# Where the four weight sums of a Strassen-Winograd down projection are made: in SBUF beside the products, or in DRAM by background transfers

## The chip, the cores and the metric

One core of a Trainium2 chip. The metric is the device time of one execution in microseconds, median of three runs; the profile is one more execution with the hardware profiler on.

## The reference

One layer on 512 tokens of width 1024, float32. A projection `h @ w_in` feeds three token mixers (gated linear attention, GLA; a causal pooling mixer; block-sparse attention, MoBA), whose outputs go through branch matrices and gates into `w_out`. Then the FFN, which is what the change is about:

```
f = (silu(h @ ffn_w_gate) * (h @ ffn_w_up)) @ ffn_w_down      # 512x1024 -> 512x2816 -> 512x1024
x = x + rmsnorm(f, norm_ffn_post)
```

## The kernel before

**Matrix products.** Each float32 operand is split into two float32r tiles, H (the rounded value, a copy on ScalarE) and L (the rest, a subtraction on VectorE), and a product is the three matmuls HH, HL, LH, accumulated in PSUM. A weight chunk of 512 KB passes through three rings of buffers: `load` (L143) allocates a buffer of `raw` (3 of them), a DMA on SyncE's queue fills it, ScalarE makes `wH` and VectorE `wL` (4 buffers each; `split_chunk`, L136). These four are marked as urgent by `LEAD`, so they run ahead of the matmuls that use them as far as the rings allow.

**Order.** The program is traced in the order of the text; a planner then puts the instructions of each engine into one fixed queue, by the text's order, the urgency marks and its own reckoning of when operands are there. At run time each engine takes its queue in order and waits where an operand is missing. Only the start (norm of x, first projections) has an order of VectorE, ScalarE and TensorE written by hand; GpSimd has there four powers for the norms (L228) and one subtraction (L326). Two GpSimd memsets of the GLA stage stand under `issue_after(pows[3].ins)`, which ties them behind the last of the four powers. In the GLA stage GpSimd squares each output (`osq`, L606) and takes a power (L610) on which VectorE's L613 waits.

**Stages in time.** Start to 30 us; projections, GLA, MoBA, pooling and branches to 432; `w_out` to 478; FFN (11 steps of 96 matmuls for gate and up) to 720; down projection to 837; the last norm and stores to 845.

**The down projection.** The product of `g` (512 x 2816) and W_down (2816 x 1024) is made as 2 x 2 quarters by the Strassen-Winograd scheme: seven products p1 to p7 of quarter size instead of eight. Quarter (z, c) of W_down has rows z*1408 on and columns c*512 on; it is loaded in six chunks (five of 2 x 128 rows, one of 128; `wq`, L885). Four of the products need a sum of quarters: t1 = (0,0) + (0,1), t2 = t1 + (1,1), t3 = (1,1) + (0,1), t4 = t2 + (1,0). The kernel before makes them so:

- t1: in the FFN stage SyncE loads (0,0) into the SBUF tiles `tau` and GpSimd issues DMAs that add (0,1) to them on landing (`plus`, L892; text at FFN steps 3 to 8).
- t2 and t4: the same tiles, by further accumulating DMAs (`t2_of`, `t4_of`), each of which waits until the splits of the sum before have read the tile.
- t3: two plain loads per chunk and an addition on VectorE (L993, L994).

The products are computed in the order p1, p2, p5, p6, p7, p3, p4 (`product`, L922). Before each, the quarter of `g` (or a sum of quarters, L972 to L988) is split by `Quarter.put` (L871). p1, p2 and p3 load their quarters into `raw` (`raw_of`, L944, L948); p5, p6 and p4 split straight from `tau`, p7 from the `t3` tiles.

Of the kernel before, what the change touches and what calls it, by code (L numbers as in the profile page):

```python
# [9 lines left out]
F32 = mybir.dt.float32  # L10
# [3 lines left out]
ALU = mybir.AluOpType  # L14
AX = mybir.AxisListType

P = 128
T = 512
# [49 lines left out]
LEAD = 400  # L68
G1W = RANK + 256
TH = T // 2  # L70
KH = NF // 2
KGROUPS = ((0, 4), (4, 8), (8, KH))
# [3 lines left out]
def hybrid_block(ctx: ExitStack, tc: tile.TileContext, a: dict, out: bass.AP):  # L76
    nc = tc.nc
    V, S, G, PE = nc.vector, nc.scalar, nc.gpsimd, nc.tensor
# [6 lines left out]
    dram = ctx.enter_context(tc.tile_pool(name="dram", bufs=1, space=bass.MemoryType.DRAM))  # L85
# [8 lines left out]
    def slot(shape, name, dt=F32):  # L94
        n = int(np.prod(shape[1:]))
        if n > D or dt != F32:
            i = free_full.pop(0)
            owner[name] = (i, None, 0)
            return big.tile(shape, dt, tag=f"S{i}", name=name, bufs=1)
        if free_half:  # L100
            i, t, lo = free_half.pop(0)
        else:
            i, lo = free_full.pop(0), 0
            t = big.tile([P, 2 * D], F32, tag=f"S{i}", name=f"two_{name}", bufs=1)
            free_half.append((i, t, D))
        owner[name] = (i, t, lo)
        ap = t[:, lo:lo + n]
        names = "abcd"[:len(shape) - 1]
        if len(shape) > 2:
            ap = ap.rearrange(f"p ({' '.join(names)}) -> p {' '.join(names)}",  # L110
                              **{c: k for c, k in zip(names, shape[1:])})
        return ap

    def free(*names):
        for name in names:
            i, t, lo = owner.pop(name)
            other = (i, t, D - lo)
            if t is None:
                free_full.append(i)
            elif other in free_half:  # L120
                free_half.remove(other)
                free_full.append(i)
            else:
                free_half.append((i, t, lo))
# [8 lines left out]
        return bass.AP(tensor=vec.tensor, offset=vec.offset, ap=[[0, P], [1, n]])  # L133


    def split_chunk(src, kt, nf, H, L, name, eng, lead):  # L136
        with tc.high_priority(offset=lead):
            raw = wpool.tile([P, kt, nf], F32, tag="raw", name=f"raw_{name}", bufs=NRAW)
            nc.sync.dma_start(raw, src.rearrange("(k p) f -> p k f", p=P))
            S.copy(H, raw)  # L140
            (eng or V).tensor_tensor(L, raw, H.bitcast(F32), op=ALU.subtract)  # L141

    def load(src, name, eng=None, lead=LEAD, keep=False):  # L143


        K, nf = src.shape[0] // P, src.shape[1]
        kt = 4 if nf == G1W else D // nf
        out = []
        for c in range(K // kt):
            if keep:  # L150
                HL = slot([P, 2, kt, nf], f"{name}_{c}", F32R)
                h, l = HL[:, 0], HL[:, 1]
            else:
                h = wpool.tile([P, kt, nf], F32R, tag="wH", name=f"wH_{name}_{c}", bufs=NWH)
                l = wpool.tile([P, kt, nf], F32R, tag="wL", name=f"wL_{name}_{c}", bufs=NWH)
            split_chunk(src[c * kt * P:(c + 1) * kt * P, :], kt, nf, h, l, f"{name}_{c}", eng, lead)
            out.append((h, l, c * kt, kt))
        return out
# [286 lines left out]
    gq, gk = gqk[:, 0], gqk[:, 1]  # L445
# [415 lines left out]
    def quarter(tz, z, i):  # L861
        return ga[z, i][:, :, tz * TH:(tz + 1) * TH]
# [15 lines left out]
        def free(self):  # L878
            free(*self.names)

    wd = a["ffn_w_down"]
    chunks = [(lo, min(lo + 2, KH)) for lo in range(0, KH, 2)]
    NG = range(len(KGROUPS))

    def wq(z, c, lo, hi):  # L885

        r = (z * KH + lo) * P
        return wd[r:r + (hi - lo) * P, c * T:(c + 1) * T].rearrange("(k p) f -> p k f", p=P)

    tau = [slot([P, hi - lo, T], f"tau{n}") for n, (lo, hi) in enumerate(chunks)]  # L890

    def plus(n, name, z, c, dst):  # L892

        nc.gpsimd.dma_start(dst, wq(z, c, *chunks[n]), accum_op=ALU.add)  # L894

    a11 = Quarter("a11")
    for u in range(NF // 2):
        W = [load(a[n][:, u * 256:(u + 1) * 256], f"{n}{u}") for n in ("ffn_w_gate", "ffn_w_up")]
        ff = [ps2((2 * u + f) % 4, f"ff{2 * u + f}") for f in range(2)]
        for lo, hi in (((0, 256), (256, 512)) if u == 0 else ((0, 512),)):  # L900
            for i in range(2):
                mm_fm([g[i][:, lo:hi] for g in ff], W[i], h2, lo, hi)
        if 3 <= u < 3 + len(chunks):
            nc.sync.dma_start(tau[u - 3], wq(0, 0, *chunks[u - 3]))
            plus(u - 3, "t1", 0, 1, tau[u - 3])
        for f in range(2):
            k = 2 * u + f
            z, r = divmod(k, KH)
            sg = t2(f"sg{k}")
            S.activation(sg, ff[f][0], AF.Silu)  # L910
            V.tensor_tensor(ga[z, r // 4][:, r % 4, :], sg, ff[f][1], op=ALU.mult)
            if z == 0 and r + 1 in [hi for _, hi in KGROUPS]:
                a11.put(r // 4, quarter(0, 0, r // 4))
    h2.free()

# [3 lines left out]
    def product(name, X, ps, src, start, group=1):  # L922

        done = []
        for n, (lo, hi) in enumerate(chunks):
            with tc.high_priority(offset=LEAD):
                w = src(n)
                h = wpool.tile([P, 2, T], F32R, tag="wH", name=f"wH_{name}{n}", bufs=NWH)[:, 0:hi - lo]
                l = wpool.tile([P, 2, T], F32R, tag="wL", name=f"wL_{name}{n}", bufs=NWH)[:, 0:hi - lo]
                S.copy(h, w)  # L930
                V.tensor_tensor(l, w, h.bitcast(F32), op=ALU.subtract)  # L931
            done.append((lo, hi, h, l))
            if n + 1 < len(chunks) and n >= len(chunks) - group:
                continue
            for j in range(2):
                for lo_, hi_, h_, l_ in done:
                    for k in range(lo_, hi_):
                        for i, (z, w_) in enumerate(((0, h_), (0, l_), (1, h_))):
                            PE.matmul(ps[j], lhsT=X.part(z, k, j), rhs=w_[:, k - lo_, :],  # L939
                                      start=start and k == 0 and i == 0, stop=k == KH - 1 and i == 2,  # L940
                                      skip_group_check=True)
            done = []

    def raw_of(z, c, name):  # L944
        def src(n):
            lo, hi = chunks[n]
            r = wpool.tile([P, 2, T], F32, tag="raw", name=f"raw_{name}{n}", bufs=NRAW)[:, 0:hi - lo]
            nc.sync.dma_start(r, wq(z, c, lo, hi))  # L948
            return r
        return src  # L950

    def t1_of(n):
        return tau[n]

    def t2_of(n):
        plus(n, "t2", 1, 1, tau[n])
        return tau[n]

    def t3_of(n):
        return t3[n]  # L960

    def t4_of(n):
        plus(n, "t4", 1, 0, tau[n])
        return tau[n]

    pa, pc, pd, pe = (ps2(i, f"p{i}") for i in range(4))
    a12 = Quarter("a12")
    for i in NG:
        a12.put(i, quarter(0, 1, i))
    s1 = [slot([P, hi - lo, TH], f"s1_{i}") for i, (lo, hi) in enumerate(KGROUPS)]  # L970
    for i in NG:
        V.tensor_tensor(s1[i], quarter(1, 1, i), quarter(1, 0, i), op=ALU.subtract)  # L972
    product("p1", a11, pa, raw_of(0, 0, "p1"), True)
    cp0 = slot([P, 2, T], "c_p")
    for j in range(2):
        S.copy(cp0[:, j], pa[j])
# [1 line left out]
    qs1 = Quarter("qs1_")  # L978
    for i in NG:
        qs1.put(i, s1[i])  # L980
    product("p2", a12, pd, raw_of(1, 0, "p2"), True)
    for j in range(2):
        V.tensor_tensor(cp0[:, j], pd[j], cp0[:, j], op=ALU.add)

# [2 lines left out]
        V.scalar_tensor_tensor(quarter(0, 0, i), s1[i], -1.0, quarter(0, 0, i), ALU.mult, ALU.subtract)  # L987
        V.scalar_tensor_tensor(quarter(0, 1, i), quarter(0, 0, i), -1.0, quarter(0, 1, i), ALU.mult, ALU.subtract)  # L988
    a12.free()
    t3 = [slot([P, hi - lo, T], f"t3_{n}") for n, (lo, hi) in enumerate(chunks)]  # L990
    for n in range(len(chunks)):
        with tc.high_priority(offset=LEAD):
            nc.sync.dma_start(t3[n], wq(1, 1, *chunks[n]))  # L993
            V.tensor_tensor(t3[n], t3[n], raw_of(0, 1, "t3")(n), op=ALU.add)  # L994
    product("p5", qs1, pc, t1_of, True)
    qs1.free()
    qs2 = Quarter("qs2_")
    for i in NG:
        qs2.put(i, quarter(0, 0, i))
    free(*[f"s1_{i}" for i in NG])  # L1000
    product("p6", qs2, pa, t2_of, False)
    qs2.free()
    qs3 = Quarter("qs3_")
    for i in NG:
# [3 lines left out]
    for j in range(2):  # L1008
        S.copy(cp1[:, j], pa[j])
        V.scalar_tensor_tensor(cp1[:, j], pc[j], -1.0, cp1[:, j], ALU.mult, ALU.subtract)  # L1010
    product("p7", qs3, pa, t3_of, False)
    qs4 = Quarter("qs4_")
    for i in NG:
        qs4.put(i, quarter(0, 1, i))
# [1 line left out]
        S.copy(cp2[:, j], pa[j])  # L1016
        V.scalar_tensor_tensor(cp2[:, j], pc[j], -1.0, cp2[:, j], ALU.mult, ALU.subtract)
    qs3.free()
    free(*[f"t3_{n}" for n in range(len(chunks))])
    product("p3", qs4, pe, raw_of(1, 1, "p3"), True)  # L1020
    a22 = Quarter("a22")
    for i in NG:
        a22.put(i, quarter(1, 1, i))
# [17 lines left out]

    for t in range(2):
        finish(t, [cp0[:, t], cp1[:, t]], (0, 1))
    product("p4", a22, pa, t4_of, False, 2)
    for t in range(2):
        finish(2 + t, [pa[t], cp2[:, t]], (1, 0))

# [26 lines left out]
```

## Time and profile before

| | |
|---|---|
| Median of 3 runs | 847.97 us (847.27 to 849.46) |
| Profiled execution | 846.82 us, its span 845.1 us |
| Busy, share of the span | TensorE 97%, VectorE 55%, ScalarE 39%, GpSimd 10% |
| Mean granted TensorE clock | 0.994 |
| DMA | 101.09 MB, mean 120 GB/s |

A share of busy time is a mean over stages with different limits, so the stages are read one by one. In the rows further on, PE is TensorE, PEld its weight loads, DVE VectorE, ACT ScalarE, POOL GpSimd, SP SyncE; SPq and POOLq are their queues of DMA issues. In an order of time a row has its start, its duration, engine, line, operation, out<-in, shape, count, and in brackets how long the engine stood idle before and what ended that. q1 is the DMA queue of SyncE, q0 that of GpSimd. Matmuls are pipelined: a single duration overlaps the next one.

### The profile page before, as it was taken

To read this page: it belongs to the slowest core of one execution; us is meant where nothing else is said; L and a number is where in the kernel's file an instruction comes from. 1 tells how busy PE (TensorE), PEld (TensorE's weight loads), DVE (VectorE), ACT (ScalarE), POOL (GpSimd) and SP (SyncE) were. 2 spreads that over 40 slices of the span, in tenths; PEclk is the share of its full clock that TensorE was granted. 3 is DMA by queue.
4 is the path that set the end of the run, shared out by engine and by line. 5 is a ranking of instruction groups with operands and counts; after the bars stand their busy time and mean duration, and the time that the engine had idled before them with its cause. 6 is when DMAs were issued, how large, how long until landed. Compare 5 with 4: busy or idle time off the path is not lost.

```text
span 845.1 us, 10322 instructions
## 1 busy us (share of the span) xinstructions
PE 821.0 (97%) x4082; PEld 694.8 (82%) x4082; DVE 461.6 (55%) x680; ACT 328.3 (39%) x496; POOL 84.1 (10%) x79
## 2 busy tenths in 40 slices
PE   6999999999999999999999999999999999996996
PEld 5888998889888877888888898888888888775785
DVE  5639967766577564334455633233323323976776
ACT  6345235454456332223344332222222222543553
POOL 3200002110010003112111120000000000012201
PEclk9999999999999999999999999999999999998999
DMA  8431221222322632333343893333333332399912
GB/s 299 125 100 51 76 75 51 74 75 72 91 75 72 217 100 75 100 100 100 99 156 120 229 229 94 97 99 100 100 99 100 93 96 89 109 251 270 263 63 100
DMA packets 77395, 101.09 MB, mean 120 GB/s; under 512 B 3730, under 2 KB 57763, under 8 KB 77347
## 3 DMA queue, kind: packets, MB, share of 16 engines
q1 hardware_dynamic: 72834, 91.78, 35.1%
q0 software_dynamic: 4512, 8.65, 5.7%
q8 instruction: 32, 0.52, 0.3%
q14 instruction: 17, 0.13, 0.0%
HBM read 96.23 MB, written 4.19 MB: 119 GB/s over the span
## 4 chain that ended last, share of the span: by engine, by line
PE 91%; DMA 4%; DVE 3%; issue 1%; ACT 0%; SPq 0%; DVEq 0%; POOLq 0%; POOL 0%; ACTq 0%
PE ff L192 28%; PE p L939 7%; PE pga L192 5%; PE pgb L192 5%; PE ow L203 5%; PE pgc L192 5%; PE mv L203 3%; PE gv L203 3%; PE pya L192 3%; PE mq L192 3%; PE pu L192 3%; PE pyb L192 3%; PE mk L192 3%; PE gqk L192 3%; PE pyc L192 3%; DMA two_t<-in_ffn_w_down_dram 2%
## 5 line engine op out<-in xcount | busy, mean ns | idle before, releaser
L141 DVE TENSOR_TENSOR wL_ffn_w_gate<-raw_ffn_w_gate,wH_ffn_w_gate 128x1024 fp32r<-128x1024 f32 x22 | 26.9, 1225 | 82.4 <-ACT wH_ffn_w_gate L140 82.2
L192 PE MATMUL ff<-h2L,wH_ffn_w_gate 128*128 128x512 f32 (+1 forms) x192 | 71.4, 372 | 0.0
L192 PE MATMUL ff<-h2L,wH_ffn_w_up 128*128 128x512 f32 (+1 forms) x192 | 71.4, 372 | 0.0
L192 PE MATMUL ff<-h2H,wL_ffn_w_up 128*128 128x512 f32 (+1 forms) x192 | 71.4, 372 | 0.0
L192 PE MATMUL ff<-h2H,wL_ffn_w_gate 128*128 128x512 f32 (+1 forms) x192 | 71.3, 372 | 0.0
L192 PE MATMUL ff<-h2H,wH_ffn_w_gate 128*128 128x512 f32 (+1 forms) x192 | 71.3, 372 | 0.0
L192 PE MATMUL ff<-h2H,wH_ffn_w_up 128*128 128x512 f32 (+1 forms) x192 | 71.2, 372 | 0.0
L939 PE MATMUL p<-wH_p,qs 128*128 128x512 f32 x176 | 56.3, 400 | 1.9 <-ACT wH_p L930 1.6
L140 ACT CAST wH_ffn_w_up<-raw_ffn_w_up 128x1024 fp32r<-128x1024 f32 x22 | 23.2, 1052 | 73.5 <-issue 35.3
L141 DVE TENSOR_TENSOR wL_ffn_w_up<-raw_ffn_w_up,wH_ffn_w_up 128x1024 fp32r<-128x1024 f32 x22 | 27.0, 1225 | 43.8 <-ACT wH_ffn_w_up L140 43.7
L894 POOL DMA_DIRECT2D two_tau<-in_ffn_w_down_dram x18 | 21.1, 1254 | 289.3 <-DVE wL_p L931 276.6
L140 ACT CAST wH_ffn_w_gate<-raw_ffn_w_gate 128x1024 fp32r<-128x1024 f32 x22 | 23.2, 1053 | 61.0 <-PE ff L192 53.1
L939 PEld LDWEIGHTS p<-wH_p,qs 128*128 128x128 f32 x176 | 34.1, 194 | 9.8 <-ACT wH_p L930 2.1
L939 PE MATMUL p<-wL_p,qs 128*128 128x512 f32 x88 | 35.7, 405 | 6.4 <-DVE wL_p L931 6.4
L192 PEld LDWEIGHTS ff<-h2L,wH_ffn_w_gate 128*128 128x128 f32 x192 | 36.2, 188 | 6.2
L192 PEld LDWEIGHTS ff<-h2L,wH_ffn_w_up 128*128 128x128 f32 x192 | 36.2, 188 | 6.2
L192 PEld LDWEIGHTS ff<-h2H,wH_ffn_w_gate 128*128 128x128 f32 x192 | 36.1, 188 | 6.3
L192 PEld LDWEIGHTS ff<-h2H,wH_ffn_w_up 128*128 128x128 f32 x192 | 36.1, 188 | 6.3
L192 PEld LDWEIGHTS ff<-h2H,wL_ffn_w_up 128*128 128x128 f32 x192 | 36.2, 188 | 6.2
L192 PEld LDWEIGHTS ff<-h2H,wL_ffn_w_gate 128*128 128x128 f32 x192 | 36.2, 188 | 6.2
L939 PE MATMUL p<-wH_p,a 128*128 128x512 f32 x132 | 41.0, 390 | 0.0
L939 PEld LDWEIGHTS p<-wH_p,a 128*128 128x128 f32 x132 | 24.8, 188 | 5.1
(338 smaller groups left out, 2080.5 us busy)
## 6 DMA issues: line engine op xcount, KB each, us to landing
raw_ffn_w_gate<-in_ffn_w_gate_dram SPq DMA_DIRECT2D x22, 512.0 KB, 3.8
raw_ffn_w_up<-in_ffn_w_up_dram SPq DMA_DIRECT2D x22, 512.0 KB, 3.8
two_tau<-in_ffn_w_down_dram POOLq DMA_DIRECT2D x15, 512.0 KB, 9.5
raw_p<-in_ffn_w_down_dram SPq DMA_DIRECT2D x15, 512.0 KB, 3.9
raw_gatea<-in_w_in_dram SPq DMA_DIRECT2D x8, 512.0 KB, 3.6
raw_gateb<-in_w_in_dram SPq DMA_DIRECT2D x8, 512.0 KB, 3.6
raw_gatec<-in_w_in_dram SPq DMA_DIRECT2D x8, 512.0 KB, 3.7
raw_wo<-in_w_out_dram SPq DMA_DIRECT2D x8, 512.0 KB, 3.4
```

Source lines behind the costliest of these rows:

```text
L140: S.copy(H, raw)
L141: (eng or V).tensor_tensor(L, raw, H.bitcast(F32), op=ALU.subtract)
L192: PE.matmul(ps, lhsT=w[:, k, f * P:(f + 1) * P], rhs=m(k0 + k, lo, hi), start=n == 0 and i == 0, stop=n == len(W) - 1 and i == len(seq) - 1)
L203: PE.matmul(ps, lhsT=m(k0 + k, lo, hi), rhs=w[:, k, c0:c1], start=first and n == 0 and i == 0, stop=last and n == len(W) - 1 and i == len( ...
L894: nc.gpsimd.dma_start(dst, wq(z, c, *chunks[n]), accum_op=ALU.add)
L939: PE.matmul(ps[j], lhsT=X.part(z, k, j), rhs=w_[:, k - lo_, :], start=start and k == 0 and i == 0, stop=k == KH - 1 and i == 2, skip_group ...
```

## The change

The four sums become DRAM tiles, `sums[t, n]`. A generator, `background`, lists 48 DMAs on GpSimd's queue: for each sum six copies DRAM to DRAM (of a quarter of W_down, or of an earlier sum) and then six accumulating transfers that add the other quarter, in the order t1, t3, t2, t4. Every call of `load` but those for gq and gk draws one of them ahead of its own instructions: 34 calls of the mixer stages, 2 of `w_out`, 12 of the FFN. No urgency mark and no `issue_after` stands around them. In the down projection all seven products load plainly into `raw`, four of them from the sums; `tau`, `t3`, L994 and the accumulations into SBUF are gone. The splits of a12 move into the FFN loop, beside those of a11.

```diff
+    sums = {(t, n): dram.tile([(hi - lo) * P, T], F32, name=f"sum{t}_{n}")
+            for t in (1, 2, 3, 4) for n, (lo, hi) in enumerate(chunks)}
+
+    def background():
+        for t, first, second in ((1, (0, 0), (0, 1)), (3, (1, 1), (0, 1)), (2, 1, (1, 1)), (4, 2, (1, 0))):
+            for n in range(len(chunks)):
+                src = sums[first, n] if type(first) is int else wq(*first, *chunks[n])
+                yield nc.gpsimd.dma_start(sums[t, n], src)
+            for n in range(len(chunks)):
+                yield nc.gpsimd.dma_start(sums[t, n], wq(*second, *chunks[n]), accum_op=ALU.add)
+
+    behind = background()
...
     def load(src, name, eng=None, lead=LEAD, keep=False):
+        if not name.startswith(("gq", "gk")):
+            next(behind, None)
         K, nf = src.shape[0] // P, src.shape[1]
...
-    tau = [slot([P, hi - lo, T], f"tau{n}") for n, (lo, hi) in enumerate(chunks)]
-
-    def plus(n, name, z, c, dst):
-
-        nc.gpsimd.dma_start(dst, wq(z, c, *chunks[n]), accum_op=ALU.add)
-
-    a11 = Quarter("a11")
+    a11, a12 = Quarter("a11"), Quarter("a12")
...
-        if 3 <= u < 3 + len(chunks):
-            nc.sync.dma_start(tau[u - 3], wq(0, 0, *chunks[u - 3]))
-            plus(u - 3, "t1", 0, 1, tau[u - 3])
...
-            if z == 0 and r + 1 in [hi for _, hi in KGROUPS]:
-                a11.put(r // 4, quarter(0, 0, r // 4))
+            if r + 1 in [hi for _, hi in KGROUPS]:
+                (a11, a12)[z].put(r // 4, quarter(0, z, r // 4))
...
-    def t2_of(n):
-        plus(n, "t2", 1, 1, tau[n])
-        return tau[n]
...
+    def sum_of(t, name):
+        return raw_of(lambda n: sums[t, n], name)
...
-    a12 = Quarter("a12")
-    for i in NG:
-        a12.put(i, quarter(0, 1, i))
...
-    t3 = [slot([P, hi - lo, T], f"t3_{n}") for n, (lo, hi) in enumerate(chunks)]
-    for n in range(len(chunks)):
-        with tc.high_priority(offset=LEAD):
-            nc.sync.dma_start(t3[n], wq(1, 1, *chunks[n]))
-            V.tensor_tensor(t3[n], t3[n], raw_of(0, 1, "t3")(n), op=ALU.add)
-    product("p5", qs1, pc, t1_of, True)
+    product("p5", qs1, pc, sum_of(1, "p5"), True)
...
-    product("p6", qs2, pa, t2_of, False)
+    product("p6", qs2, pa, sum_of(2, "p6"), False)
...
-    product("p7", qs3, pa, t3_of, False)
+    product("p7", qs3, pa, sum_of(3, "p7"), False)
...
-    product("p4", a22, pa, t4_of, False, 2)
+    product("p4", a22, pa, sum_of(4, "p4"), False, 2)
```

## Rows read from the trace of the kernel before

**Rows 1.** The page's first part: busy us, share, instructions of TensorE.
```profile
PE 821.0 (97%) x4082; PEld 694.8 (82%) x4082; DVE 461.6 (55%) x680; ACT 328.3 (39%) x496; POOL 84.1 (10%) x79
```

**Rows 2.** Stretches: length; busy PE, PEld, DVE, ACT, POOL; clock; DMA share; GB/s.
```profile
0.00:25.00 25.00, 16.94 (x107) 16.16 (x108) 14.78 (x29) 15.15 (x31) 11.06 (x14) 1.00 0.77 265
25.00:50.00 25.00, 25.00 (x124) 20.82 (x122) 11.01 (x18) 7.83 (x11) 0.76 (x1) 1.00 0.48 136
50.00:116.00 66.00, 66.00 (x463) 61.41 (x463) 54.80 (x70) 30.11 (x36) 0.00 (x0) 1.00 0.20 57
488.00:720.00 232.00, 232.00 (x1082) 194.59 (x1081) 73.79 (x71) 63.96 (x74) 3.95 (x4) 1.00 0.38 106
```

**Rows 3.** TensorE's waits behind 600 us (total, times, longest); the first.
```profile
PE p L939 <- DVE wL_p L931: 7.6, 4, 4.2
PE p L939 <- ACT wH_p L930: 1.6, 1, 1.6
739.67 0.50 PE L939 MATMUL p<-wL_p,a 128*128 128x512 f32 x1 [1.25 <-DVE wL_p L931]
```

**Rows 4.** Stretches of 6 us in the down projection, columns as above.
```profile
734.00:740.00 6.00, 4.75 (x20) 3.36 (x19) 6.00 (x7) 5.62 (x7) 0.00 (x0) 1.00 0.42 139
776.00:782.00 6.00, 3.17 (x8) 2.50 (x9) 6.00 (x7) 0.78 (x1) 1.25 (x2) 0.56 1.09 273
782.00:788.00 6.00, 6.00 (x25) 4.91 (x24) 5.10 (x6) 3.23 (x4) 4.53 (x4) 0.87 1.02 216
806.00:812.00 6.00, 6.00 (x28) 4.99 (x27) 5.78 (x7) 4.36 (x7) 0.00 (x0) 1.00 0.66 218
```

**Rows 5.** VectorE's waits, 720 to 845 us, and one addition in time.
```profile
DVE two_t L994 <- DMA two_t<-in_ffn_w_down_dram: 6.5, 2, 3.9
DVE two_t L994 <- DMA raw_t<-in_ffn_w_down_dram: 6.3, 3, 4.4
775.28 1.23 DVE L994 TENSOR_TENSOR two_t<-two_t,raw_t 128x1024 f32<-128x1024 f32 x1 [3.91 <-DMA two_t<-in_ffn_w_down_dram]
```

**Rows 6.** DMA queues from 738 to 800 us: GpSimd's queue (packets, MB, share).
```profile
q0 software_dynamic: 3008, 5.77, 52.0%
```

**Rows 7.** DMA queues over the whole span (the page).
```profile
q1 hardware_dynamic: 72834, 91.78, 35.1%
q0 software_dynamic: 4512, 8.65, 5.7%
```

**Rows 8.** The products' plain loads (KB, us to landing); one copy.
```profile
raw_p<-in_ffn_w_down_dram SPq DMA_DIRECT2D x15, 512.0 KB, 3.9
739.04 1.05 ACT L930 CAST wH_p<-raw_p 128x1024 fp32r<-128x1024 f32 x1
```

**Rows 9.** SyncE's queue in order of time, from the start.
```profile
6.61 0.38 SPq L139 DMA_DIRECT2D raw_gq<-in_w_in_dram  x1
12.33 0.38 SPq L795 DMA_DIRECT2D pw<-in_pool_w_dram  x1
```

**Rows 10.** GpSimd's waits (total, times, longest); two places in time.
```profile
POOL rs_m L228 <- DVE ms_m L226: 10.1, 3, 5.0
POOL wL_g1r L326 <- ACT wH_g1r L324: 3.2, 1, 3.2
116.44 1.04 POOL L606 TENSOR_TENSOR osq<-osb 128x512 f32<-128x512 f32 x1 [90.67 <-ACT osb L605]
490.23 2.12 POOL L894 DMA_DIRECT2D two_tau<-in_ffn_w_down_dram  x2 [0.37 <-issue]
```

**Rows 11.** Line 894, the accumulations: ns min/median/max, and landing.
```profile
L894 POOL DMA_DIRECT2D two_tau<-in_ffn_w_down_dram x18: 899/1203/1691, 463.3 to 785.8; - x18
DMA to landing us min/median/max: 5.6/9.4/12.1
```

**Rows 12.** The last chain's first piece; ScalarE's copy of gq.
```profile
2.58 5.78 DMA raw_g1r<-in_w_in_dram
18.10 1.04 ACT L140 CAST wH_gq<-raw_gq 128x1024 fp32r<-128x1024 f32 x1
```

More of the change, by code (lines that the diff above doesn't have):

```diff
@@ L133, in rows, with wq @@
         return bass.AP(tensor=vec.tensor, offset=vec.offset, ap=[[0, P], [1, n]])
+    wd = a["ffn_w_down"]
+    chunks = [(lo, min(lo + 2, KH)) for lo in range(0, KH, 2)]
+    def wq(z, c, lo, hi):
+        r = (z * KH + lo) * P
+        return wd[r:r + (hi - lo) * P, c * T:(c + 1) * T]
+    sums = {(t, n): dram.tile([(hi - lo) * P, T], F32, name=f"sum{t}_{n}")
[8 more added lines that the diff above has]
+    behind = background()
     def split_chunk(src, kt, nf, H, L, name, eng, lead):
@@ L879, in free @@
             free(*self.names)
-    wd = a["ffn_w_down"]
-    chunks = [(lo, min(lo + 2, KH)) for lo in range(0, KH, 2)]
     NG = range(len(KGROUPS))
-    def wq(z, c, lo, hi):
-        r = (z * KH + lo) * P
-        return wd[r:r + (hi - lo) * P, c * T:(c + 1) * T].rearrange("(k p) f -> p k f", p=P)
-    tau = [slot([P, hi - lo, T], f"tau{n}") for n, (lo, hi) in enumerate(chunks)]
-    def plus(n, name, z, c, dst):
-        nc.gpsimd.dma_start(dst, wq(z, c, *chunks[n]), accum_op=ALU.add)
-    a11 = Quarter("a11")
+    a11, a12 = Quarter("a11"), Quarter("a12")
     for u in range(NF // 2):
@@ L942, in product, with raw_of @@
             done = []
-    def raw_of(z, c, name):
+    def raw_of(ap_of, name):
         def src(n):
@@ L947, in src, with quarter_of @@
             r = wpool.tile([P, 2, T], F32, tag="raw", name=f"raw_{name}{n}", bufs=NRAW)[:, 0:hi - lo]
-            nc.sync.dma_start(r, wq(z, c, lo, hi))
+            nc.sync.dma_start(r, ap_of(n).rearrange("(k p) f -> p k f", p=P))
             return r
         return src
-    def t1_of(n):
-        return tau[n]
-    def t2_of(n):
-        plus(n, "t2", 1, 1, tau[n])
[L957 to L964, printed above, removed]
+    def quarter_of(z, c, name):
+        return raw_of(lambda n: wq(z, c, *chunks[n]), name)
+    def sum_of(t, name):
+        return raw_of(lambda n: sums[t, n], name)
     pa, pc, pd, pe = (ps2(i, f"p{i}") for i in range(4))
-    a12 = Quarter("a12")
-    for i in NG:
-        a12.put(i, quarter(0, 1, i))
     s1 = [slot([P, hi - lo, TH], f"s1_{i}") for i, (lo, hi) in enumerate(KGROUPS)]
@@ L972, in hybrid_block @@
         V.tensor_tensor(s1[i], quarter(1, 1, i), quarter(1, 0, i), op=ALU.subtract)
-    product("p1", a11, pa, raw_of(0, 0, "p1"), True)
+    product("p1", a11, pa, quarter_of(0, 0, "p1"), True)
     cp0 = slot([P, 2, T], "c_p")
@@ L980, in hybrid_block @@
         qs1.put(i, s1[i])
-    product("p2", a12, pd, raw_of(1, 0, "p2"), True)
+    product("p2", a12, pd, quarter_of(1, 0, "p2"), True)
     for j in range(2):
@@ L1018, in hybrid_block @@
     qs3.free()
-    free(*[f"t3_{n}" for n in range(len(chunks))])
-    product("p3", qs4, pe, raw_of(1, 1, "p3"), True)
+    product("p3", qs4, pe, quarter_of(1, 1, "p3"), True)
     a22 = Quarter("a22")
```

## The prediction

> **What bounds the kernel now.** The first thing to read is the share of busy time: TensorE has 97% of the span [rows 1]. The number of matmuls does not change, so all that can be won is time in which TensorE waits or is clocked down. I looked for it stage by stage with a table of stretches [rows 2]: from 25 us on TensorE is busy without a break at a granted clock of 1.00, up to the end of the FFN at 720 us (three such stretches stand there). What is left is the start, which waits for loads, and the down projection. There the list of waits gives 7.6 us in four waits for VectorE's splits and 1.6 us in one for ScalarE's [rows 3]. Behind the longest, of 4.2 us, the clock is granted at 0.56 for 6 us and 0.87 for the next 6 [rows 4]; an undisturbed stretch of 6 us holds 28 matmuls, so the 8 + 25 matmuls there are worth 33 x 6/28 = 7.1 us and took 3.17 + 6.00 = 9.2: 2.1 us. The down projection has 9.2 + 2.1 = 11.3 us to give, and no other stage behind the start anything.
>
> The reader should see two causes in it. The first wait (1.25 us at 739, the one for ScalarE soon behind) falls where VectorE is busy 6.00 of 6 us [rows 3, 4]: its own work. At the later ones it is idle for much of the time, and its waits say why: the additions for t3 (L994) stand 6.5 + 6.3 = 12.8 us before loads that have not landed [rows 5], and the splits (L931) that TensorE needs are queued behind them. The DMA share is then above 1.0 [rows 4], and more than half of it is the 12 accumulating transfers [rows 6].
>
> **The change, part by part.**
>
> *Down projection, removed.* The additions L994 (five of 1.23 us and a half one [rows 5], 6.8 us of VectorE) and the accumulating transfers of t2 and t4: 5.77 MB at 52.0% of 62 us, 32 us of all 16 engines [rows 6]. As plain loads, which go at 91.78 MB in 35.1% of 845.1 us, 309 GB/s [rows 7], they are 19 us. The three later waits and the clock dip go: 7.6 - 1.25 + 2.1 = 8.5 us. The other two (2.9 us) stay: up to there VectorE loses only splits of a12, which now go into the FFN, where it is 32% busy [rows 2], and of those one group waits for the last FFN tile in any case.
>
> *Down projection, added.* p5, p6, p7 and p4 now load through the ring of three raw buffers. A load lands in 3.9 us (median) and its copy takes 1.05 [rows 8]; its subtraction takes what an addition of L994 takes, 1.23: 6.2 us per buffer, 2.1 us per chunk with three. TensorE needs 12 matmuls per chunk, 12 x 6/28 = 2.6 us. So the ring holds, with 0.5 us per chunk to spare; p3 already runs so, with TensorE at 6.00 of 6 us in the slice that begins at 806 [rows 4]. But p5's loads now stand behind p2's, whose buffers VectorE frees late. Cost between 0 and the 2.9 us that the two waits show for such lateness; I take 1.0. Gain of the down projection: 8.5 - 1.0 = 7.5 us (bounds 4 to 11).
>
> *The background transfers: where will they run?* There are 48 on GpSimd's queue: four sums of six copies and six accumulations. In the text one goes with each load from gv on. The trace says that the text's position holds no instruction back. pw (L795) stands behind sixteen loads that would each carry a transfer, is used only in the pooling mixer, and is issued at 12.33 us [rows 9]. On GpSimd the accumulations of t1 stand in the text at FFN steps 3 to 8; step 3 begins 8 steps of 96 matmuls, 8 x 96 x 6/28 = 165 us, before 720; the last of them are issued at 490 us [rows 10], when their loads had landed. An instruction is issued when its engine is free and its inputs are there. The copies read inputs only and write fresh DRAM tiles. GpSimd stands idle before the start's powers 10.1 us in three pieces (5.0, 3.2, 1.9) and 3.18 us before the split [rows 10], and an issue holds it 1.20 us [rows 11]: 4 + 2 + 1 + 2 = 9 transfers before the last power at 19 us. I take this: the background begins at the start, not in the mixer.
>
> *Its price at the start.* No row shows a DRAM to DRAM transfer. Nearest rows per 512 KB: the plain 309 GB/s, 1.70 us of the 16 engines, and the accumulations' 8.65 MB in 5.7% of 845.1 us, 179 GB/s, 2.92 us [rows 7]. In the first 25 us the engines are busy 77% [rows 2], so nine transfers push 15 to 26 us of work into a stretch with 5.7 us free. What TensorE waits for there is loads: the chain begins with the first weight load, 5.78 us [rows 12]. Cover: gq's first chunk is issued at 6.61 and copied at 18.10 us [rows 9, 12], with the 5.78 us of such a load some 4 us in hand besides its wait behind the loads issued before it. Taking the copies' price, since the first six are plain: 9 x 1.70 - 4 = 11 us. Bounds: 0 (all of it beside other waits) and 26. TensorE does not idle later, so a late start is not given back.
>
> The Trainium skill, "DMA: Bandwidth & Descriptors", section "Anatomy of one DMA — SWDGE (gpsimd) path", gives a transfer issued from GpSimd as 2.0 us plus its bytes at 436 GB/s: 3.2 us for 512 KB, 1.2 of it movement. By that the nine would cost 9 x 1.2 - 4 = 7 us, and with the gain of 7.5 the start would come out even. The trace disagrees: landing 9.4 us median, 179 GB/s [rows 7, 11], so I do not follow it.
>
> *Its price behind the start.* GpSimd takes its queue in order, and an accumulation waits there for its copy to land. Behind it stand the powers at the start, and at 116 us osq [rows 10] and the power of oss, on which VectorE waits at once (L613). All 48 (22 x 512 KB copied, as much accumulated) are 22 x 1.70 + 22 x 2.92 = 101 us of the 16 engines, up to 128; free are 0.23 x 25 + 0.52 x 25 + 0.80 x 66 = 72 us up to 116 us [rows 2]. So osq finds the queue in use. At least 0 (if the order leaves gaps that fit), at most the third rival below; I take 4 us.
>
> *Other edits.* The FFN loses its tau loads and six accumulations; TensorE shows no gap there, so nothing.
>
> **Sum.** The profiled execution took 846.82 us, 845.1 of it span; the median of the runs is 847.97, 1.15 more. 846.8 - 7.5 + 11 + 4 = 854.3, on the median's scale 855.5: I say 855.
>
> **Rivals.**
> 1. *Spread as the text has it* (36 transfers one per load up to w_out, 12 in the FFN). For: the DMA share there is 0.20 to 0.48 [rows 2], so they are hidden; against: rows 9 and 10. The gain of 7.5 stays, less about 1 us where an issue of 1.20 stands ahead of osq or oss: 840.3, 841 on the median's scale. Faster.
> 2. *At the start, but cheaply*: the weight load at the head of the chain shares with the copies and takes up to twice its 5.78 us; the rest catches up, as from 25 to 50 us half the engines are free. 846.8 - 7.5 + 6 = 845.3, 846.5: the same.
> 3. *GpSimd's queue decides*: all accumulations are ordered ahead of osq and each waits for a copy in a backlog. By the 72 us free of 101, 29 us of work are left at 116, with 0.80 free some 36 us more. TensorE has splits and projections in hand for part of it; I count 30 in all, with the start's 11 inside: 846.8 - 7.5 + 30 = 869.3, 870. It decides where the planned order took transfers for quicker than they are; the down projection shows that it can, by VectorE's 12.8 us before L994 [rows 5].
>
> **Chances.** The forecast 0.40, rival 1 0.24, rival 2 0.16, rival 3 0.20. Differences under about 0.3% (2.5 us) cannot be told from none. Slower: most of the forecast (0.33), rival 3 (0.20), a little of rival 2 (0.02): 0.55. The same: 0.05 of the forecast, 0.03 of rival 1, 0.08 of rival 2: 0.16. Faster: 0.02 + 0.21 + 0.06 = 0.29. Range: from a little under rival 1 (838) to beyond rival 3 (885), which leaves out the low end of rival 1 and the start's upper bound together with rival 3. The forecast's own range is 849 to 866.
>
> **What would show it.** In the profile after: (a) the first background transfers on GpSimd before 10 us. If the first stands behind 30 us, rival 1 holds and I am wrong. (b) The first weight load lands later than 8.4 us (2.58 + 5.78), and the gq matmuls begin some 11 us later than now. (c) osq behind a transfer's wait on GpSimd; over 10 us there means rival 3. (d) Between 747 us and the last matmul, moved by the late start, no wait of TensorE over 1 us and the clock at 1.00; waits of ScalarE's copies for raw loads that reach TensorE there would mean that the ring does not hold.

## The result and the profile after

The kernel after takes 871.46 us (median of 4 runs, 870.31 to 872.94) where the kernel before took 847.64 beside it (847.27 to 849.46): a ratio of 1.0278, 95% interval 1.0255 to 1.0300, or 23.8 us slower. The forecast was 855. The direction and the wide range (838 to 885) held. The forecast's own range (849 to 866) did not: by its sum the kernel loses 7.5 us, and it loses 23.8.

The page of the kernel after, its busy time and its DMA queues (packets, MB, share of 16 engines), to be held against [rows 1, 7]:

```profile
PE 824.5 (95%) x4082; PEld 698.6 (80%) x4082; DVE 455.6 (52%) x674; ACT 327.0 (38%) x496; POOL 97.3 (11%) x109
q1 hardware_dynamic: 74338, 94.67, 35.5%
q0 software_dynamic: 8000, 23.07, 10.9%
```

TensorE has as many matmuls as before and the span is 25.1 us longer (870.2 against 845.1), so TensorE waits more or runs slower. The page doesn't say where; landmarks do. The last matmul of gk, which closes the first projections, in the kernel before and then in the kernel after (ns min/median/max, first and last start):

```profile
L192 PE MATMUL gqk<-hTH,wL_gk x16: 388/389/390, 39.4 to 49.6; 128*128 128x512 f32 x16
```
```profile
L218 PE MATMUL gqk<-hTH,wL_gk x16: 389/389/632, 73.0 to 85.0; 128*128 128x512 f32 x16
```

It stands at 85.0 instead of 49.6: 35.4 us late. The table gives the same for later landmarks, and for the experiments below.

| start of, us | last gk matmul | last gr matmul | first w_out matmul | last FFN matmul |
|---|---|---|---|---|
| before | 49.6 | 97.6 | 432.2 | 719.7 |
| after | 85.0 | 137.7 | 470.1 | 757.5 |
| e1, all transfers behind the start | 50.8 | 98.8 | 440.9 | 728.3 |
| e2, transfers of 16 rows | 65.7 | 113.7 | 448.3 | 735.8 |
| e10, eight copies at the start | 62.6 | 109.0 | 448.8 | 736.3 |
| e11, spread as the text | 50.2 | 98.3 | 432.8 | 728.7 |
| e3, all at the FFN's start | 50.9 | 98.9 | 433.5 | 741.7 |
| e4, five per FFN step | 50.1 | 98.1 | 432.7 | 720.2 |

The kernels with no transfer ahead of the start's fourth power (before, e1, e3, e4, e11) have their last gk matmul between 49.6 and 50.9, so a landmark is good to about 1 us.

So 35.4 us are lost before 85 us, some 2.5 more by w_out (37.9), and nothing in the FFN. In the down projection the products' first matmul starts at 757.8 and their last at 862.8, 105.1 us later; before, these were 719.9 and 838.2, 118.3 us: 13.2 back. 37.9 - 13.2 = 24.7, which is the 25.1 of the span but for 0.4.

**The start.** GpSimd's queue in order of time (start, us, engine, line, operation, count, and the idle time before with what ended it):

```profile
1.27 4.66 POOL L153 DMA_DIRECT2D sum<-in_ffn_w_down_dram  x8 [0.44 <-issue]
10.89 0.56 POOL L153 DMA_DIRECT2D sum<-in_ffn_w_down_dram  x1 [4.96 <-DMA sum<-in_ffn_w_down_dram]
15.65 0.52 POOL L153 DMA_DIRECT2D sum<-in_ffn_w_down_dram  x1 [1.26 <-DMA sum<-in_ffn_w_down_dram]
16.28 0.59 POOL L254 TENSOR_TENSOR rs_m<-ms_m,half 128x1 f32<-128x1 f32 x1
49.94 0.56 POOL L254 TENSOR_TENSOR rs_m<-ms_m,half 128x1 f32<-128x1 f32 x1 [11.68 <-DVE ms_m L252]
147.21 1.04 POOL L632 TENSOR_TENSOR osq<-osb 128x512 f32<-128x512 f32 x1 [37.40 <-ACT osb L631]
```

Eight copies go out at once; the ninth stands 4.96 us until the first has landed, and three more follow in the same way. Behind all twelve stands the first power, at 16.28. Its input was there at 6.2 (VectorE's L252 runs from 6.03), and VectorE waits for it (10.7 us) and TensorE behind VectorE. The fourth power comes at 49.94 instead of 19.3, but its last wait is for VectorE and not for a transfer. The second cost is in the DMA. The queues from 0 to 25 us, before and then after:

```profile
q1 hardware_dynamic: 5307, 6.60, 77.2%
```
```profile
q0 software_dynamic: 1360, 4.95, 56.4%
q1 hardware_dynamic: 1693, 2.68, 32.9%
```

SyncE's loads moved 6.60 MB in that time and move 2.68 beside the transfers: the transfers hold 56.4% of the engines' time, the loads 32.9%. ScalarE shows what this does (in order of time):

```profile
20.04 1.10 ACT L350 CAST wH_g1r<-raw_g1r 128x1088 fp32r<-128x1088 f32 x1 [14.04 <-DMA raw_g1r<-in_w_in_dram]
44.63 1.04 ACT L164 CAST wH_gq<-raw_gq 128x1024 fp32r<-128x1024 f32 x1 [10.82 <-DMA raw_gq<-in_w_in_dram]
45.58 1.06 ACT L341 CAST hTH<-tp_m 128x512 fp32r<-128x512 f32 x2
```

The first weight chunk is copied at 20.04 (8.39 before). Then the copy of gq waits 10.82 us for its load, and behind it in ScalarE's fixed order stands hTH, which needs no load: the late load also holds work that was ready. SyncE's own queue stretches as well; two issues in order of time, where one took 0.38 us before [rows 9]:

```profile
5.36 3.99 SPq L315 DMA_DIRECT2D two_x<-in_x_dram  x1
13.84 2.46 SPq L163 DMA_DIRECT2D raw_gq<-in_w_in_dram  x1
```

The chain of work that ended last (start, us, what) goes through this load, not through GpSimd, which has no piece of it up to 85 us:

```profile
13.84 30.77 DMA raw_gq<-in_w_in_dram
44.63 1.04 ACT wH_gq L164
45.68 0.49 ACT hTH L341
```

The late first power is covered too: TensorE's first g1r matmul (21.68 instead of 10.03) waits for hTH, which stands behind the copy of the first weight chunk.

TensorE's waits of the kernel after (total, times, longest), the first three before 60 us, the fourth at 128 us. Before, the first stood at 7.5, the second at 0.5, and the others were not in the list:

```profile
PE tp_m L335 <- DVE two_wpre L332: 17.7, 1, 17.7
PE g1r L366 <- ACT hTH L341: 11.8, 2, 9.8
PE g1r L366 <- ACT wH_g1r L350: 5.9, 1, 5.9
PE sps L567 <- DVE qhat L562: 2.7, 1, 2.7
```

These are 38.1 us against 8.0, so some 30 of the 37.9 are waits. The rest, some 8 us, are matmuls that ran slower. Two stretches (columns as in [rows 2]):

```profile
25.00:50.00 25.00, 9.14 (x40) 8.21 (x39) 6.99 (x13) 6.26 (x13) 6.38 (x8) 0.80 1.11 255
50.00:75.00 25.00, 25.00 (x141) 21.10 (x140) 11.53 (x21) 9.52 (x16) 13.10 (x16) 0.97 1.10 293
```

The 0.80 is a mean: TensorE stood still from 36.4 to 46.2 us, and from 42 to 48 it was granted 0.50, the lower of its two levels (1.2 and 2.4 GHz). Before, the clock was 1.00 there.

**The down projection.** Three stretches of 6 us of it and of the last FFN work (columns as in [rows 4]), and its only wait over 0.2 us, which answers to [rows 3]:

```profile
734.00:740.00 6.00, 6.00 (x28) 4.99 (x27) 5.96 (x7) 2.11 (x2) 0.00 (x0) 1.00 0.23 86
793.90:799.90 6.00, 6.00 (x28) 4.97 (x27) 1.17 (x2) 1.67 (x2) 0.00 (x0) 1.00 0.88 287
811.90:817.90 6.00, 5.86 (x26) 4.50 (x24) 3.75 (x5) 4.44 (x6) 0.00 (x0) 1.00 0.81 264
```
```profile
PE p L947 <- ACT two_s L1001: 0.3, 1, 0.3
```

No wait for a split is left, and the clock is granted at 1.00 in each of them.

### The profile page after: what moved, and what is told of

Its sections match the earlier page's. It is cut to its first block, busy times and chain, and to the rows that moved or that the text cites. A ratio compares the mean times of both kernels' runs of the same rounds, so it can differ in the third digit from the quotient of the medians.

```text
span 870.2 us, 10358 instructions
## 1 busy us (share of the span) xinstructions
PE 824.5 (95%) x4082; PEld 698.6 (80%) x4082; DVE 455.6 (52%) x674; ACT 327.0 (38%) x496; POOL 97.3 (11%) x109
## 3 DMA queue, kind: packets, MB, share of 16 engines
q0 software_dynamic: 8000, 23.07, 10.9%
## 4 chain that ended last, share of the span: by engine, by line
PE 89%; DMA 6%; DVE 2%; SPq 1%; issue 1%; ACT 1%; DVEq 0%; POOLq 0%; POOL 0%; ACTq 0%
PE ff L218 28%; PE p L947 12%; PE pga L218 5%; PE pgb L218 5%; PE ow L229 5%; PE pgc L218 5%; DMA raw_gq<-in_w_in_dram 4%; PE gqk L218 3%; PE mv L229 3%; PE pya L218 3%; PE pu L218 3%; PE mq L218 3%; PE pyb L218 3%; PE mk L218 3%; PE pyc L218 3%; DMA raw_mv<-in_w_in_dram 2%
## 5 line engine op out<-in xcount | busy, mean ns | idle before, releaser
L939 DVE TENSOR_TENSOR wL_p<-raw_p,wH_p 128x1024 fp32r<-128x1024 f32 (+1 forms) x42 | 47.2, 1133 | 30.9 <-ACT wH_p L938 30.7
L938 ACT CAST wH_p<-raw_p 128x1024 fp32r<-128x1024 f32 (+1 forms) x42 | 41.1, 980 | 52.4 <-PE p L947 22.4
L254 POOL TENSOR_TENSOR rs_pf<-ms_pf,half 128x1 f32<-128x1 f32 x4 | 3.4, 840 | 340.8 <-DVE ms_pf L252 340.8
```

The source lines that it names most:

```text
L254: pows.append(G.tensor_tensor(rs, ms, half[:, 0:1], op=ALU.pow))
```

## The experiments

Each was timed in alternation with the kernel before, whose medians in the three batches were 847.66, 847.12 and 847.34; its single runs went from 841.9 to 849.7. The open question was the start: is it the bytes, or GpSimd's queue, or both? And why does the down projection win more than forecast?

**Everything behind the start.** All transfers tied behind the fourth power:

```diff
-            next(behind, None)
+            with tc.issue_after(pows[3].ins):
+                next(behind, None)
```

> The transfers are tied behind the fourth power of the start, so none is issued before about 20 us; all else is the changed kernel. Theory A (the transfers take the 16 DMA engines from the weight loads for as long as they run, the loads keep about a third): the start up to 20 us is as before the change, but the loads of 20 to 130 us still land in 14 us and more, so some of the loss stays: 843 to 856 us. Theory B (the loss is GpSimd's own queue: the start's powers and split stand behind transfers that wait): nothing of it is left, the gain of the down projection (13 us) shows in full: 833 to 837 us.

Measured: 843.57 us, ratio 0.9956 (0.9941 to 0.9971). That is 27.9 us less than the kernel after, with the same 48 transfers on the same queue; only when they start differs. The last gk matmul is back at 50.8. From 20 to 128 us the transfers hold 75.6% of the engines and gv's and the following loads land in 11 to 21 us (gv's in 3.6 before), yet TensorE loses nothing up to gr: the loads run ahead by the rings, and there is time in hand then. The rest of the kernel pays once, at osq. GpSimd in order of time, and the wait of TensorE that hangs on it:

```profile
126.70 0.81 POOL L155 DMA_DIRECT2D sum<-in_ffn_w_down_dram  x1 [0.26 <-DMA sum<-sum]
127.25 1.33 POOL L633 TENSOR_TENSOR osq<-osb 128x512 f32<-128x512 f32 x1
```
```profile
PE ytp L643 <- DVE osb L640: 5.6, 1, 5.6
```

This is the mechanism of the third rival, in the place where it was put, at some 7.5 us (8.7 late at w_out, 1.2 at gr). The time lies in theory A's range, but not for A's reason: the late loads cost nothing up to gr.

**The queue without the bytes.** The transfers cut to 16 rows, 32 KB; the products load plain quarters, so the sums are left out of the result:

```diff
-                yield nc.gpsimd.dma_start(sums[t, n], src)
+                yield nc.gpsimd.dma_start(sums[t, n][0:16], src[0:16])
...
-    product("p5", qs1, pc, sum_of(1, "p5"), True)
+    product("p5", qs1, pc, quarter_of(0, 0, "p5"), True)
```

> The same 48 transfers at the start in the same queue, each cut to its first 16 rows (32 KB in place of 512), and p5, p6, p7 and p4 load plain quarters in place of the sums (the four sums are left out of the result). Theory A: with the bytes gone the loss goes, and only the gain of the down projection is left: 833 to 838 us. Theory B: the powers still stand behind transfers that wait for a landing; a landing is then 2 to 3 us, a dozen of them ahead of the second power: 845 us or more.

Measured: 851.19 us, 1.0042 (1.0027 to 1.0057). The last gk matmul stands at 65.7: 16.1 us late, and so is w_out. GpSimd in order of time, and TensorE's waits:

```profile
10.66 0.93 POOL L254 TENSOR_TENSOR rs_m<-ms_m,half 128x1 f32<-128x1 f32 x1
14.21 8.52 POOL L155 DMA_DIRECT2D sum<-in_ffn_w_down_dram  x10
22.69 1.65 POOL L254 TENSOR_TENSOR rs_m<-ms_m,half 128x1 f32<-128x1 f32 x1
```
```profile
PE tp_m L335 <- DVE two_wpre L332: 15.5, 1, 15.5
PE tp_m L335 <- DVE two_hn L332: 6.2, 3, 3.5
```

The powers come at 10.66, 22.69, 26.27 and 35.55 where they came at 5.84, 12.17, 14.65 and 19.32. Ten accumulations are issued in a row, 8.52 us, and the second power stands behind them. So the place in GpSimd's queue costs 16.1 us with hardly any bytes (0.85 MB in the first 25 us, 16.7% of the engines), as theory B said; the clock, 0.89 from 25 to 50 us, has its part in it.

**The bytes without the queue.** Eight copies at the start, as many as go out without a wait, and the rest behind the fourth power (the copies of t1 and t3 put first in the list):

```diff
-            next(behind, None)
+            nth[0] += 1
+            if nth[0] <= 8:
+                next(behind, None)
+            else:
+                with tc.issue_after(pows[3].ins):
+                    next(behind, None)
```

> Eight copies stay at the start, where GpSimd would be idle anyway and none of them waits; the other 40 transfers are tied behind the start's fourth power as in the run that held all. So the start has the bytes of eight transfers (3.9 MB, some 16 us of the engines) and next to no queue. If the bytes at the start cost by themselves: 10 to 18 us more than with all held (843.6), 853 to 862 us. If only the queue on GpSimd costs there: 843 to 846 us.

Measured: 849.25 us, 1.0036 (1.0018 to 1.0054). The first power in time, TensorE's first waits, and the landmark:

```profile
6.26 0.57 POOL L263 TENSOR_TENSOR rs_m<-ms_m,half 128x1 f32<-128x1 f32 x1 [0.35 <-DVE ms_m L261]
```
```profile
PE tp_m L344 <- DVE two_wpre L341: 12.0, 1, 12.0
PE g1r L375 <- ACT hTH L350: 7.9, 1, 7.9
```
```profile
L227 PE MATMUL gqk<-hTH,wL_gk x16: 388/389/389, 52.4 to 62.6; 128*128 128x512 f32 x16
```

The power is on time (6.26, after VectorE and not after a DMA), and still the last gk matmul is 13.0 us late. The late first loads do it: the first g1r matmul, which needs the copy of the first weight chunk, is 11.8 us late already (21.83 instead of 10.03). The total, 849.25, falls between the two ranges expected, so neither theory holds alone: either cost is there without the other, 16.1 us for the queue and 13.0 for the bytes of eight copies.

The two don't simply add up to the 35.4 of the kernel after. There the loads are the later of the two, by the chain above, and cover what GpSimd's queue holds up; and they land later than here, with twenty transfers issued before the last power instead of eight. How the 35.4 would fall if only one of the two were taken away, no run shows. (The marker has a small fault of its own: in the kernel after, all eight lg matmuls, 1.9 us of work, stand ahead of the last gk matmul, in the others behind it.)

**Spread as the text.** Each transfer tied behind the last GpSimd instruction of the text before its load, the first rival made true:

```diff
-            next(behind, None)
+            with tc.issue_after(recent[0].ins):
+                next(behind, None)
```

> Each transfer stays with its load, but tied behind the last GpSimd instruction that the text has traced before it, so that it can't move ahead of its stage: the spread over the mixer stages that the text shows. If both costs (bytes beside the start's loads, the queue ahead of GpSimd's work) come from the bunching: 834 to 838 us. If transfers beside the mixer's loads cost wherever they stand: 842 us or more.

Measured: 843.21 us, 0.9962 (0.9945 to 0.9979). That is in the range of the second expectation, but nothing is lost through the mixers (0.6 us at w_out's start): the last FFN matmul is 9.0 us late, and most of that is lost at w_out. Waits of TensorE and ScalarE there, and the loads of w_out (KB, us to landing), which took 3.4 us before:

```profile
PE ow L231 <- ACT wo L165: 5.3, 2, 4.9
```
```profile
ACT wo L165 <- DMA raw_wo<-in_w_out_dram: 17.2, 3, 7.1
```
```profile
raw_wo<-in_w_out_dram SPq DMA_DIRECT2D x8, 512.0 KB, 7.6
```

Six accumulations, tied behind masks of the stage before, fall between 400 and 450 us, beside w_out's loads (2.88 MB, 40.2% of the engines). Besides the wait of 5.3 us the clock is granted at 0.86 from 444 to 456. The first rival's 841 thus was near, for a kernel that wins 13.2 and loses 9.0.

**One burst in the FFN.** All 48 behind the last power ahead of the FFN, where GpSimd has nothing behind them:

```diff
+    with tc.issue_after(pows[-1].ins):
+        for _ in behind:
+            pass
```

> All 48 transfers are tied behind the last power ahead of the FFN, so they run in one burst from about 483 us on, where GpSimd has nothing else to do. Theory A: the FFN's loads get about 100 GB/s beside the burst, as the start's loads did, and need 96, so a loss of 0 to 10 us of TensorE's time in the FFN and the gain of 13 us in the down projection: 834 to 845 us. Theory B: no work of GpSimd stands behind the transfers, so no loss: 833 to 836 us.

Measured: 855.27 us, 1.0103 (1.0076 to 1.0129): slower, and outside both ranges expected, although the FFN has free engines enough over its length. The queues from 485 to 600 us, TensorE's longest wait, and the loads' landing:

```profile
q0 software_dynamic: 7863, 22.84, 83.4%
q1 hardware_dynamic: 6894, 6.85, 21.6%
```
```profile
PE ff L216 <- ACT wH_ffn_w_gate L164: 11.6, 2, 6.3
```
```profile
raw_ffn_w_gate<-in_ffn_w_gate_dram SPq DMA_DIRECT2D x7, 512.0 KB, 20.7
```

6.85 MB in 115 us are 60 GB/s for the loads; the FFN draws 94 (22.81 MB in 242 us in the next run). TensorE falls 20.7 us behind, with no GpSimd work held: 12.6 us of waits for weights in the FFN, the rest at a clock granted at 0.83 to 0.88 from 540 to 600 us. It is the burst that costs, not the amount, as the next run shows.

**Five per FFN step.** The same 48, tied in fives behind a one-column GpSimd copy of what each step has just made:

```diff
+            if f == 1 and u < 10:
+                mark = G.tensor_copy(tick[:, u:u + 1], ga[z, r // 4][:, r % 4, 0:1])
+                with tc.issue_after(mark.ins):
+                    for _ in range(5):
+                        next(behind, None)
```

> The 48 transfers go five per FFN step, each group tied behind a one-column copy on GpSimd that needs the step's result, so they are spread over the FFN. The transfers of a step are some 9 to 12 us of the engines in 21.8 us, the loads some 8. Both theories: no loss at the start, none or up to 2 us in the FFN, and the gain of 13 us in the down projection: 833 to 837 us, faster than both kernels. A gain of 7.5 us or less (840 or more) would say that the gain measured in the changed kernel hangs on something in its mixer stages.

Measured: 834.81 us, 0.9857 (0.9834 to 0.9881): the best version, 12.9 us under the kernel before and 36.7 under the kernel after. The queues from 478 to 720 us:

```profile
q0 software_dynamic: 8000, 23.07, 41.4%
q1 hardware_dynamic: 21193, 22.81, 30.7%
```

Each group of five moves 2.4 MB in a step of 22 us. Loads still land late (10.0 us median for the up weights, 4.4 for the gate), but the rings cover it: TensorE has no wait in the FFN, and the down projection keeps its whole 13.2.

**Where the 13.2 come from.** Two runs on the version of e4, first with a12's splits put back behind the FFN loop, then with three SBUF slots also kept occupied where `tau` had been:

```diff
-            if r + 1 in [hi for _, hi in KGROUPS]:
-                (a11, a12)[z].put(r // 4, quarter(0, z, r // 4))
+            if z == 0 and r + 1 in [hi for _, hi in KGROUPS]:
+                a11.put(r // 4, quarter(0, 0, r // 4))
     h2.free()
+    for i in NG:
+        a12.put(i, quarter(0, 1, i))
```

> The kernel with five transfers per FFN step (834.8), with a12's splits put back behind the FFN loop, as before the change. If the first two waits of the down projection (1.25 and 1.64 us before) went because a12's splits moved: both come back, 836.5 to 839 us. If they went for another reason: 834 to 836 us.

```diff
+    held = [free_full.pop(0) for _ in range(3)]
     a11 = Quarter("a11")
...
     h2.free()
+    a12 = Quarter("a12")
```

> The run with a12 late, and three SBUF slots taken away where tau had them, a12 in slots that come free behind the FFN, as before the change. If the two waits went because the slots of tau came free, so that the sums of quarters of g could be made earlier: they come back here, with VectorE busy without a break from the end of the FFN on, 836.5 to 839 us. If they went because of the additions and accumulations: 834 to 836 us here too.

Measured: 834.54 us (0.9862, 0.9834 to 0.9889), no change against e4; and 836.77 (0.9886, 0.9853 to 0.9919), 2.2 us more. With the slots held, the first wait of [rows 3] is back (TensorE, then VectorE in order of time):

```profile
741.19 0.50 PE L955 MATMUL p<-wL_p,a 128*128 128x512 f32 x1 [1.22 <-DVE wL_p L947]
722.21 3.23 DVE L977 TENSOR_TENSOR two_s<-ga,ga 128x1024 f32<-128x1024 f32 x3
```

So the text's place of a12 is worth nothing; what frees VectorE is that sums of `g` which need an SBUF slot find one during the FFN once `tau` is gone. With the slots held, all three sums of L977 run behind the FFN, as before the change; in e5 only the last of them does (721.44). The second early wait, for ScalarE, does not come back in e6: why that one went is not shown.

Then two runs on the kernel before, one without the additions for t3 (t3 is then (1,1) alone, and the six loads of the other quarter go too), one without the accumulations of t2 and t4 (p6 and p4 then use t1):

```diff
-            V.tensor_tensor(t3[n], t3[n], raw_of(0, 1, "t3")(n), op=ALU.add)
```

> The kernel before, with t3 made of its first quarter alone: the six loads of the other quarter and the six additions L994 are left out (so is that term of the sum). If the down projection's later waits came from VectorE's queue standing at L994 for late loads: they go, 838 to 841 us, though the 12 accumulations stay. If the accumulations hold p6's sums back by themselves: part of the waits stays, 842 to 846 us.

```diff
-        plus(n, "t2", 1, 1, tau[n])
...
-        plus(n, "t4", 1, 0, tau[n])
```

> The kernel before, without the 12 accumulations of t2 and t4 (p6 and p4 use t1; those terms are left out), with t3's loads and additions kept. If the accumulations' 32 us of the engines are what made t3's loads late: the later waits go here as well, 838 to 841 us. If 11 loads of t3 beside p2's and p3's are late by themselves: most of the waits stay, 843 to 847 us.

Measured: 838.43 us (0.9894, 0.9879 to 0.9908) and 839.86 (0.9908, 0.9890 to 0.9926). Both keep the two early waits and lose all three later ones; TensorE of the first in order of time:

```profile
740.30 0.50 PE L939 MATMUL p<-wL_p,a 128*128 128x512 f32 x1 [1.22 <-DVE wL_p L931]
747.37 0.73 PE L939 MATMUL p<-wH_p,qs 128*128 128x512 f32 x2 [1.34 <-ACT wH_p L930]
```

Taking away either half is enough: the later waits needed both the accumulations, which made t3's loads late, and the additions of VectorE standing before these loads, with the splits behind.

## Why the prediction was right in direction and wrong in size

- **Where the transfers run: right.** They begin at 1.27 us, ahead of everything, as read from pw's early issue [rows 9]. Sign (a) came as written.
- **The sum's start term, "9 x 1.70 - 4 = 11": the step that failed.** The mechanism (transfers take the engines from the start's loads) and the price of a copy were right: e10's eight copies took 48.9% of 25 us for 3.93 MB, 1.6 us of the engines per 512 KB. The count was wrong: I filled the idle time of GpSimd that [rows 10] show with issues of 1.20 us. A copy takes 0.5 to 0.8, eight go out at once, and the order puts twelve copies ahead of the first power and eight accumulations ahead of the last. By 44.6 us, when gq's load lands, the transfers had used 28 us of the engines (63.4% of the time, 7.89 MB), not 15. The 4 us of cover were not there either: I took 5.78 us for gq's first load, which took 9.7 in the kernel before and so had 1.8 in hand, and the first chunk of g1r had none.
- **A cost put at nothing: the clock.** The sum has no term for what TensorE loses at a lower granted clock behind long waits. That is some 8 of the 37.9 us.
- **"GpSimd's queue behind the start, 4 us, at osq": the right resource in the wrong place.** I named the powers of the start as standing behind the transfers, but let them run on time, as if transfers went only into idle gaps. In the fixed order transfers stand before them, and without the bytes that is worth 16.1 us (e2). At osq the kernel after loses nothing: osq waits for ScalarE at 147 us, and the queue has been free since 110. Sign (c) did not come. In e1, where TensorE is on time, it does.
- **Together:** 15 us forecast for the start and the queue, 37.9 measured. They go with late loads in the chain of the kernel after; the part that GpSimd's queue would have by itself in it stays open. Sign (b) came larger: gq's first matmul 31.2 us late (24.1 to 55.3), not 11.
- **The third rival's 870 is near the result, but not its mechanism.** It counted a backlog that holds osq; all but some 2.5 us of the loss was there by the last gk matmul, so its number is luck. Its "the planned order took transfers for quicker than they are" fits what was seen, without being tested.
- **Work on the DMA engines: right.** All transfers took 23.07 MB at 10.9% of 870.2 us, 95 us of 16 engines (243 GB/s); the forecast had 101.
- **The down projection, 7.5 forecast, 13.2 measured.** The later waits and the clock: 8.5 forecast; e7, which is rid of them, is 8.9 us faster than the kernel before, and in its trace the products take 9.8 us less (108.5 instead of 118.3). p5's loads: 1.0 forecast, no wait seen. The two early waits, 2.9, were said to stay and went: I moved only a12's splits and missed that `tau`'s slots come free. e6 brings back the first of them (its products take 1.8 us more than e4's 105.1); why the second went stays open. Sign (d) came as written.

In the first 25 us of the kernel after, GpSimd's transfers held 56.4% of the 16 engines and SyncE's loads 32.9%; in e3 it was 83.4% to 21.6%. The Trainium skill, "DMA: Bandwidth & Descriptors", section "Issuing engines are not separate DMA queues", says that DMAs started by the scalar, sync or gpsimd engine all run on the same 16 DMA engines and interleave there; the traces agree.

## What to carry to other kernels

In this program a transfer that depends on nothing was issued as early as its queue allowed, whatever its place in the text: tie it to something that happens when there is room, and read off the first rows of its queue what it stands before. Free engine time over a long stage is no cover against a burst; the same 23 MB cost 20.7 us in one burst and nothing at five transfers per step. When a change gives buffers back, ask what work had been waiting for them. And when TensorE is made to wait, look at its clock behind the wait as well.

## What the runs showed of the hardware

- Between GpSimd's transfers and SyncE's loads the engines were not shared evenly: loads kept about a third (32.9% in the first 25 us) down to a fifth (21.6% in e3), and the first projections' landed in 14 to 27 us (medians) instead of 3.6 to 7.5.
- Where both queues had work they moved about as many packets as each other, 1877 and 1874 from 25 to 50 us of the kernel after and 7863 and 6894 from 485 to 600 us of e3. GpSimd's packets were larger, 2.1 KB against 1.3 and 2.9 KB against 1.0, and with them its share of the engines.
- SyncE's issues of loads, 0.3 to 0.8 us in the kernel before, took up to 7.8 us in the first 40 us beside the transfers (six of them 2.4 us or more); a load of 16 KB landed after 28.7 us instead of 9.6.
- In these programs GpSimd issued eight transfers without a wait; the ninth stood until the first had landed, 4.96 us at 512 KB and 0.97 at 32 KB.
- TensorE's granted clock was 0.50 (1.2 GHz) from 42 to 48 us in the kernel after, where TensorE had stood still from 36.4 to 46.2; up to w_out the matmuls took some 8 us longer than in the kernel before, where it was 1.00.
